# A second pass with results in five half tiles, two sets of down-projection sums made ahead, and memory work dealt out among the attention blocks

## The chip, the cores and the metric

One core of a Trainium2 chip runs the whole kernel. The metric is device time in microseconds (us), the median of the runs. Five engines take part, each with an instruction queue of its own that is worked off in order: PE (TensorE, matmuls), DVE (VectorE), ACT (ScalarE), POOL (GpSimd) and SP (SyncE), which in this kernel issues all the DMAs.

## The reference

One layer of a streaming encoder for 2048 prompt frames and 32 sample frames, width 1024, in float32:

```python
hp = rmsnorm(xp, g_pre_mix)
qa, ka, va, qb, kb, vb, la, r = mix_inputs(hp, w_in, ...)       # one projection
oa = chunk_band_prompt(qa, ka, va, rel_bias)                     # 8 heads x 64, band of 9 chunks
ob, sp = gla_recurrence(qb, kb, vb, la, s0, GLA_BLOCK)           # 4 heads, gated linear attention
xp = xp + rmsnorm(mix_output(oa, ob, r, g_gla_out, w_o), g_post_mix)
mk, mv = mem_kv(mem_prompt, g_mem, w_mk, w_mv)                   # 256 memory rows
xp = xp + rmsnorm(mem_attention(rmsnorm(xp, g_pre_mem), mk, mv, w_mq, w_mo), g_post_mem)
xp = xp + rmsnorm(swiglu(rmsnorm(xp, g_pre_ffn), w_gate, w_up, w_down), g_post_ffn)   # hidden 2816
```

The sample frames go the same way with caches. Keys and values of the memory, the recurrence's states and the last attention keys and values are outputs too.

## The kernel before

**Arithmetic.** A float32 product is made as three products of fp32r halves, hi x hi, hi x lo and lo x hi (`mm3`). `split` makes the halves: ACT casts the high one (L459), DVE or POOL subtracts for the low one (L460); `split_own` does so in place (L464, L465). Large products use a seven-product scheme, so that weights are added and subtracted in sevens ahead of the matmuls.

**Order.** The kernel's instructions are recorded, and `class Order` then plans the issue order of every engine by a list schedule with estimated costs in several passes. The order in which the code is written sets priorities only. What the planner fixes is the order in each engine's queue; at run time each queue waits for what its first instruction needs.

**Stages**, with the time in the profiled execution of before:

- 0 to 535: projections.
- 535 to 1119: band attention and GLA in four blocks of tokens. PE's short attention products are mixed with "dense" steps, taken from a list `dense` with one entry for each block: for block 0 the memory keys (`mkps`) and `keys_fold` of the four memory heads (`gps`), for blocks 1 to 3 the out-projection of the block before (`wops`, which multiplies w_o with `om`, the mixer's output that is stored to `od` and loaded again). A number beside each entry paces its steps.
- 1119 to 1149: the memory values (`vals`: eight groups `mvps` of 24 matmuls, each copied out by DVE as `mvf`, L1510, from the pool `pd`, which has one PSUM bank).
- 1149 to 1231: the last out-projection woven with `values_fold(h)` for the four heads. `values_fold` multiplies the head's values `vt` with pieces of w_mo (`wov`) into `hps`, copies that to `hst` (DVE and ACT in turn, L1555) and stores it to `hd`. Beside it `score_weights` prepares the next stage.
- 1231 to 1405: scores of the memory attention.
- 1405 to 1632: the second pass, `output(i, pT)` for eight tiles of 256 tokens. A tile loads its probabilities `pT`, which are split in place, multiplies them with `hT` (`mo`, 192 matmuls), copies the four banks into `y` (`my`, ACT, L1874), norms, adds x1, stores x2, norms again and stores h2 (`h2d<-my`). The pool "by" has two buffers for y, 8 KB each for a partition, so tile i+2's first copy waits until tile i's last store has landed. Between the tiles `sums_out` makes the FFN's down-projection sums of set 0 (`down_pair(0)`: `wdr` is loaded, added and subtracted, split into `wds`, stored to `wdd`).
- 1632 to 3012: the FFN in three blocks of tokens (`pg`, `pu`, `pdX/Y/Z`). Block 0 makes the sums of the sets that are not in `MADE`, uses them and stores them to `wdd` for the other blocks. Set 4 is made in the projection stage.

The junction between attention and out-projection is a chain: `g_tt` (PE transposes the last GLA outputs), `g_sg` (DVE), the store to `od`, the load of `om` (L1102), ACT's cast and POOL's subtract for each of eight `om`, then `wops`.

The lines that the change speaks of:

```python
dense = [(steps(kv + [partial(keys_fold, h) for h in range(HM)]), 1 + 8 * 2 + 5 * HM), ...]
...
for _ in steps(vals):
    pass
...
for _ in steps(outp[3][0] + weave(outp[3][1], [partial(values_fold, h) for h in range(HM)], lead=1.0)):
    pass
...
yp = pool("by", 2)
y = yp.tile([P, KT, 256], F32, tag="y", name=f"my{i}")
MADE = (0, 4,)
```

Of the kernel before, what the change touches and what calls it, by code (L numbers as in the profile page):

```python
# [9 lines left out]
F32 = mybir.dt.float32  # L10
F32R = mybir.dt.float32r
AF = mybir.ActivationFunctionType
ALU = mybir.AluOpType
# [5 lines left out]
P = 128  # L19
D = 1024  # L20
KT = D // P
# [408 lines left out]
def encoder_step(ctx, tc, ins, outs):  # L430
    nc = tc.nc
    ACT, DVE, POOL, SP = nc.scalar, nc.vector, nc.gpsimd, nc.sync
# [17 lines left out]
    gains = {}  # L450
# [80 lines left out]
    HM = 4  # L531
# [16 lines left out]
    HK = KT // 2  # L548
# [93 lines left out]
    with ExitStack() as ph:  # L642
        def pool(name, bufs, **kw):
            return ph.enter_context(tc.tile_pool(name=name, bufs=bufs, **RW, **kw))
# [7 lines left out]
        wrp = pool("pwr", 4)  # L652
# [374 lines left out]
        bufs = []  # L1027
# [9 lines left out]
        items, raw = quarters(0, True)  # L1037
# [3 lines left out]
        for b in range(len(PB)):  # L1041
# [15 lines left out]
            if b + 1 < len(PB):  # L1057
                items, raw = quarters(b + 1)
# [13 lines left out]
    with ExitStack() as ph, ExitStack() as dn:  # L1072
# [6 lines left out]
        sp = pool("as", 2, dn)  # L1079
# [6 lines left out]
        up = pool("au", 4, att, **RT)  # L1086
        gp = pool("ag", 1, att, **RT)
        pd = pool("apd", 1, space=PSUM)
        pm = pool("apm", 2, apm, space=PSUM)
# [433 lines left out]
        def fold_head(src, h, nm):  # L1523
            t = kvs[-1].tile([P, 2, 544], F32R, tag="xw", name=f"{nm}{h}")[:, :, :512]
            SP.dma_start(t[:, 1].bitcast(F32).rearrange("p (j n) -> p j n", j=2), src[h * 256 : h * 256 + 256, :].rearrange("(j p) n -> p j n", p=P))
            split_own(t, True)
            return t
# [4 lines left out]
        def keys_fold(h):  # L1532
            kt = fold_head(mkd, h, "kt")
            for a in range(2):
                w = fold_w(ins["w_mq_t"], h, a, "wqt")
                for i2 in range(2):
# [7 lines left out]
                    SP.dma_start(gd[a][h // 2].rearrange("p (k n) -> p k n", k=HK)[:, 2 * i2 : 2 * i2 + 2, c0 : c0 + NMEM], g.rearrange("p (i n) -> p i n", i=2))  # L1544
                    yield

        def values_fold(h):
            vt = fold_head(mvd, h, "vt")
            for a in range(2):
                w = fold_w(ins["w_mo"][0], h, a, "wov")  # L1550
                for t in range(2):
                    ps = psc.tile([P, 512], F32, tag="X", name=f"hps{h}{a}{t}", bufs=2)
                    mm3(ps, [((vt[:, 0, j * NMEM + t * P : j * NMEM + t * P + P], vt[:, 1, j * NMEM + t * P : j * NMEM + t * P + P]), (w[j][0][:, 0], w[j][1][:, 0])) for j in range(2)])
                    hv = sp.tile([P, 544], F32, tag="st", name=f"hst{h}{a}{t}")[:, :512]
                    (ACT.copy if t else DVE.tensor_copy)(hv, ps)  # L1555
                    SP.dma_start(hd[(2 * h + t) * P : (2 * h + t + 1) * P, a * 512 : a * 512 + 512], hv)
                    yield


        def steps(items):  # L1560

            for it in items:
                r = it()
                if r is not None:
                    yield from r
                yield
# [27 lines left out]
        fin_at = [0] + [fin_at[4 * b + 3] for b in range(NB - 1)] + [len(order)]  # L1594
        kv, vals = mem_kv()
        outp = [out_proj(b) for b in range(NB)]
        dense = [(steps(kv + [partial(keys_fold, h) for h in range(HM)]), 1 + 8 * 2 + 5 * HM), (steps(outp[0][0] + outp[0][1]), 25), (steps(outp[1][0] + outp[1][1]), 25), (steps(outp[2][0] + outp[2][1]), 25)]
        ends = starts[1:] + [total]
        FIN = {0: (0,), 1: (1, 2), 2: (3, 4), 4: (5,), 5: (6, 7), 6: (8, 9)}
        DSTART, DEND = (6, 4, 7, 7), (0, 0, 0, 7)  # L1600
# [42 lines left out]
            for _ in gen:  # L1643
                pass
        states_out()
        for _ in steps(vals):
            pass
        axs.close()
        att.close()
# [5 lines left out]
        psc = pool("bpc", 1, pss, **RP)  # L1655
# [27 lines left out]
                SP.dma_start(s6d[:, k * 512 : k * 512 + 512], b21)  # L1683

        score_weights()
        for _ in steps(outp[3][0] + weave(outp[3][1], [partial(values_fold, h) for h in range(HM)], lead=1.0)):
            pass
        psx.close()
        amm.close()
# [11 lines left out]
        for i, src in ((5, gd[1][0]), (6, s6d)):  # L1701
            raw = weight_of(i)
# [103 lines left out]
        wrp = pool("bcr", 4, **RT)  # L1806
        hps_ = [pool(f"bh{q}", 1, **RT) for q in range(4)]
        tps = [pool(f"bt{q}", 1, **RT) for q in (2, 3, 0, 1)]
        yp = pool("by", 2)
        sp = pool("bs", 2)  # L1810
        side = Tagged(raw=wrp, sum=pool("bcs", 6), down=pool("bcd", 4))
        spacer("gap1", 4352, left=True)
        side.pools.update(u=pool("bcu", 3), stage=pool("bct", 3))
        pn = pool("bpm", 2, **RP)
# [2 lines left out]
        for q in range(4):  # L1817
            t = hps_[q].tile([P, 2, 2, D], F32R, tag="h", name=f"hT{q}")
# [14 lines left out]

        def output(i, pT):
            t0 = i * 256
            y = yp.tile([P, KT, 256], F32, tag="y", name=f"my{i}")
            pair = lambda m2: y[:, 2 * m2 : 2 * m2 + 2]
            ssq = {}

            def square(m2, nm):  # L1840
                if m2 == 0:
                    ssq[nm] = sp.tile([P, 2, 256], F32, tag="ssq", name=f"{nm}s{i}")
                    ACT.activation(ssq[nm], pair(0), AF.Square)
                else:
                    sq = sp.tile([P, 2, 256], F32, tag="sq", name=f"{nm}q{i}_{m2}")
                    ACT.activation(sq, pair(m2), AF.Square)
                    add(DVE, ssq[nm], ssq[nm], sq)

            def rstd(nm):
                r = (pd.tile([P, 512], F32, tag="dense", name=f"{nm}{i}") if nm == "n3_" else ptr.tile([P, 512], F32, tag="tr", name=f"{nm}{i}"))[:, :256]  # L1850
                add(DVE, ssq[nm][:, 0], ssq[nm][:, 0], ssq[nm][:, 1])
                PE.matmul(r, lhsT=ones, rhs=ssq[nm][:, 0], start=True, stop=True)
                ACT.activation(r, r, AF.Ln, bias=eps_t, scale=1.0 / D)
                ACT.activation(r, r, AF.Exp, scale=-0.5)
                return r

            def store(dst, m2):
                for b, lo, hi, off in pieces(CB, t0, t0 + 256):
                    SP.dma_start(dst[b][2 * m2 * P : (2 * m2 + 2) * P, lo:hi].rearrange("(k p) n -> p k n", p=P), pair(m2)[:, :, off : off + hi - lo])

            def scaled(m, g, r):
                DVE.scalar_tensor_tensor(out=y[:, m], in0=y[:, m], scalar=gains[g][:, m : m + 1], in1=r, op0=ALU.mult, op1=ALU.mult)

            banks = (pn, py) if i == NQ - 1 else pys
            for m4 in range(2):
                pss = [banks[m4].tile([P, 512], F32, tag="norm" if banks[m4] is pn else "out", name=f"mo{i}_{2 * m4 + j}") for j in range(2)]
                for e in range(2):
                    for hf in range(2):
                        for j in range(2):
                            c = slice((4 * m4 + 2 * j + e) * P, (4 * m4 + 2 * j + e) * P + P)  # L1870
                            mm3(pss[j][:, e * 256 : e * 256 + 256], [((hT[hf * HK + k][:, 0, c], hT[hf * HK + k][:, 1, c]), (pT[hf][:, 0, k], pT[hf][:, 1, k])) for k in range(HK)], hf == 0, hf == 1)
                for j in range(2):
                    m2, ps = 2 * m4 + j, pss[j]
                    ACT.copy(pair(m2), ps.rearrange("p (e n) -> p e n", e=2))  # L1874
                    square(m2, "n3_")
            yield
            r = rstd("n3_")
            (b, lo, _, _), = pieces(BLK, t0, t0 + 256)
            for m2 in range(KT // 2):
                xr = sp.tile([P, 2, 256], F32, tag="xr", name=f"x1r{i}_{m2}", bufs=3)  # L1880
                SP.dma_start(xr, x1d[b][2 * m2 * P : (2 * m2 + 2) * P, lo : lo + 256].rearrange("(k p) n -> p k n", p=P))
                for m in (2 * m2, 2 * m2 + 1):
                    scaled(m, "g_post_mem", r)
                add(POOL, pair(m2), pair(m2), xr)
                store(x2d, m2)
                square(m2, "n4_")
            yield
            r = rstd("n4_")
            for m2 in range(KT // 2):
                for m in (2 * m2, 2 * m2 + 1):  # L1890
                    scaled(m, "g_pre_ffn", r)
                store(h2d, m2)
# [94 lines left out]
        def sums_out():  # L1987
            for j in MADE[:-1]:
                yield from (it() for it in down_pair(j, lambda name: [side.tile([P, 2, 512], F32R, tag="down", name=f"{name}_{q}") for q in range(4)], lambda n, name: side.tile([P, 2, 512], F32R, tag="sum", name=name)))

        MADE = (0, 4,)
        own, sums = sample(), sums_out()
        last, pT = None, probs_of(0)
        for i in range(NQ):
# [13 lines left out]
    with ExitStack() as ph:  # L2008
# [4 lines left out]
        uu = pool("cu", UB)  # L2013
        gp = pool("cg", 4)
        np_ = pool("cn", 1)
        xp = pool("cx", 2)
        mps = {i: pool(f"cm{i}", 1) for i in range(7)}
        wr = pool("cwr", WRB, **RT)
# [3 lines left out]
        sp = pool("cs", 4, **RT)  # L2022
# [11 lines left out]
        pd = Turns([pool("cpd0", 3, space=PSUM, **RT), pool("cpd1", 3, space=PSUM)], 3)  # L2034
# [79 lines left out]
        with tc.high_priority(offset=PRI):  # L2114
            raw = {}
# [8 lines left out]
        for b, (s, n) in enumerate(CF):  # L2124
# [40 lines left out]
            def down_sums(j):  # L2165

                w = {}
                with tc.high_priority(offset=PRI):
                    if b or j in MADE:
                        for i in XYZ:  # L2170
# [167 lines left out]
            for g in range(NG):  # L2338
# [3 lines left out]
                if not last and g == NG - 2:  # L2342
                    raw = ffn_raw(b + 1, 0)
# [91 lines left out]
```

## Time and profile before

| what | before |
|---|---|
| median of 3 runs | 3011.1 us (3009.85 to 3013.73) |
| profiled execution | 3014.34 us, span of its instructions 3012.6 us |
| PE busy | 2936.7 us (97%), 20995 matmuls |
| DVE, ACT, POOL busy | 2263.5, 1593.8, 838.3 us |
| mean granted TensorE clock | 0.992 |
| moved by DMA | 578.90 MB, mean 192 GB/s |

Idle time of an engine matters only where the engine that sets the end waits for it. The median and the profiled execution are different executions, so a sum worked out from the trace is set against the trace's own time first.

### The profile page before, as it was taken

Reading aid. Unit: us, or ns where it says so; the run is one execution under the profiler, and the core shown is the slowest. Engines: PE = TensorE matmul, PEld = TensorE weight load, DVE = VectorE, ACT = ScalarE, POOL = GpSimd, SP = SyncE. Lnnn points to the kernel's source line nnn. Section 1 sums busy time; section 2 is a strip of 40 time slices with the busy share of each in tenths; the row PEclk is TensorE's granted clock in tenths of the full one; section 3 lists DMA queues with packets and bytes.
Section 4 is the critical chain, followed back from the end, with each engine's and each line's share of the span. In section 5 each row is a group of like instructions: output and inputs, shape, how many; then the busy total and the mean of one; then the engine's idle time right before and its main releaser. Section 6 shows DMA issues by size and latency. Waiting matters only on the chain.

```text
span 3012.6 us, 56389 instructions
## 1 busy us (share of the span) xinstructions
PE 2936.7 (97%) x20995; PEld 2758.1 (92%) x20995; DVE 2263.5 (75%) x4173; ACT 1593.8 (53%) x3389; POOL 838.3 (28%) x987
## 2 busy tenths in 40 slices
PE   9999999999999998999999999999999999999997
PEld 7899999888887777888989999999999999999997
DVE  6588876566776777874667888889977778977775
ACT  5555555676776665565435544445433335433343
POOL 0201000556767463221221111114211113311113
PEclk9999999999999999999999999999999999999999
DMA  9567374996775769546773544454454445544434
GB/s 319 197 202 239 115 232 154 302 304 196 244 246 187 214 214 313 176 156 220 260 241 112 183 149 155 165 182 162 152 195 129 136 153 174 177 164 139 132 127 169
DMA packets 429636, 578.90 MB, mean 192 GB/s; under 512 B 48720, under 2 KB 321081, under 8 KB 429329
## 3 DMA queue, kind: packets, MB, share of 16 engines
q1 hardware_dynamic: 429361, 575.29, 58.4%
q8 instruction: 165, 2.70, 0.4%
q14 instruction: 110, 0.90, 0.1%
HBM read 419.12 MB, written 160.33 MB: 192 GB/s over the span
## 4 chain that ended last, share of the span: by engine, by line
PE 88%; DMA 4%; DVE 4%; ACT 2%; issue 1%; POOL 1%; SPq 0%; DVEq 0%; ACTq 0%; POOLq 0%
PE pu_X L500 8%; PE pg_X L500 8%; PE pdX L500 8%; PE mo L500 5%; PE wops L1426 5%; PE pu_Y L500 4%; PE pg_Y L500 4%; PE pdY L500 4%; PE msX L500 3%; PE pu_Z L500 2%; PE s L1154 2%; PE pg_Z L500 2%; PE po L1162 2%; PE pdZ L500 2%; PE pt L1182 2%; PE pdn L500 1%
## 5 line engine op out<-in xcount | busy, mean ns | idle before, releaser
L460 POOL TENSOR_TENSOR u<-g,u 128x692 fp32r<-128x692 f32 (+1 forms) x111 | 200.0, 1808 | 901.7 <-ACT u L459 872.7
L500 PE MATMUL pg_X<-mf,wg_s 128*128 128x346 f32 (+1 forms) x1584 | 278.4, 323 | 1.2 <-DVE g L555 1.2
L500 PE MATMUL pu_X<-mf,wu_s 128*128 128x346 f32 (+1 forms) x1584 | 276.5, 322 | 0.9 <-ACT pu_c L638 0.8
L500 PEld LDWEIGHTS pg_X<-mf,wg_s 128*128 128x128 f32 x1584 | 256.8, 189 | 3.3 <-DVE g L555 1.7
L500 PEld LDWEIGHTS pu_X<-mf,wu_s 128*128 128x128 f32 x1584 | 256.7, 189 | 1.6 <-ACT pu_c L638 1.5
L500 PE MATMUL pdX<-u,wd 128*128 128x346 f32 (+1 forms) x1440 | 233.2, 322 | 0.0
L500 PEld LDWEIGHTS pdX<-u,wd 128*128 128x128 f32 x1440 | 230.5, 189 | 0.0
L459 ACT CAST wg_s<-wg_r 128x512 fp32r<-128x512 f32 x231 | 136.2, 620 | 176.0 <-DVE wg_r L552 80.3
L1426 PE MATMUL wops<-om,wo_s 128*128 128x512 f32 (+1 forms) x960 | 215.8, 362 | 8.2 <-ACT wo_s L459 4.7
L459 ACT CAST u<-g 128x692 fp32r<-128x692 f32 (+1 forms) x111 | 84.3, 774 | 221.2 <-PE pdX L500 165.0
L500 PE MATMUL mo<-pT,hT 128*128 128x256 f32 x1536 | 195.2, 287 | 6.0 <-ACT my L1874 3.9
L500 PEld LDWEIGHTS mo<-pT,hT 128*128 128x128 f32 x1536 | 189.2, 194 | 12.6 <-ACT my L1874 4.9
L460 DVE TENSOR_TENSOR wu_s<-wu_r,wu_s 128x512 fp32r<-128x512 f32 x231 | 172.8, 774 | 25.7 <-ACT wu_s L459 25.5
L460 DVE TENSOR_TENSOR wg_s<-wg_r,wg_s 128x512 fp32r<-128x512 f32 x231 | 160.6, 718 | 34.1 <-ACT wg_s L459 34.0
L459 ACT CAST wu_s<-wu_r 128x512 fp32r<-128x512 f32 x231 | 136.7, 620 | 88.2 <-DVE wu_r L552 37.3
L1426 PEld LDWEIGHTS wops<-om,wo_s 128*128 128x128 f32 x960 | 152.6, 189 | 30.9 <-ACT wo_s L459 5.7
L500 PE MATMUL pg_Y<-mf,wg_s 128*128 128x346 f32 (+1 forms) x792 | 139.0, 322 | 4.9 <-ACT my L1874 3.2
L500 PE MATMUL pu_Y<-mf,wu_s 128*128 128x346 f32 (+1 forms) x792 | 138.1, 322 | 2.4 <-ACT wu_s L459 2.4
L555 DVE TENSOR_TENSOR acc<-acc,pdX 128x346 f32<-128x346 f32 (+1 forms) x192 | 96.9, 513 | 57.4 <-PE pdX L500 57.2
L500 PEld LDWEIGHTS pg_Y<-mf,wg_s 128*128 128x128 f32 x792 | 128.1, 189 | 6.1 <-ACT my L1874 3.5
L500 PEld LDWEIGHTS pu_Y<-mf,wu_s 128*128 128x128 f32 x792 | 128.0, 188 | 3.1 <-ACT wu_s L459 3.0
L1341 POOL TENSOR_TENSOR g_W<-g_W,g_kq 128x128 f32<-128x128 f32 x224 | 108.6, 519 | 56.2 <-ACT g_W L1333 55.9
(561 smaller groups left out, 7186.1 us busy)
## 6 DMA issues: line engine op xcount, KB each, us to landing
wd<-wdd SPq DMA_DIRECT2D x168, 512.0 KB, 5.3
wg_r<-in_w_ffn_gate_dram SPq DMA_DIRECT2D x66, 512.0 KB, 4.2
wu_r<-in_w_ffn_up_dram SPq DMA_DIRECT2D x66, 512.0 KB, 4.6
wdd<-wd SPq DMA_DIRECT2D x42, 512.0 KB, 3.2
q<-qd SPq DMA_DIRECT2D x32, 512.0 KB, 5.4
wo_r<-in_w_o_dram SPq DMA_DIRECT2D x64, 256.0 KB, 3.8
nb<-nbd SPq DMA_DIRECT2D x16, 640.0 KB, 7.3
ks<-kad SPq DMA_DIRECT2D x20, 512.0 KB, 6.5
```

The source lines that it names most:

```text
L459: ACT.copy(hi, src)
L460: (lo_eng or DVE).tensor_tensor(out=lo, in0=src, in1=hi.bitcast(F32), op=ALU.subtract)
L500: PE.matmul(ps, lhsT=a, rhs=b, start=first and i == 0, stop=last and i == len(seq) - 1, skip_group_check=skip)
L555: eng.tensor_tensor(out=out, in0=a, in1=b, op=ALU.add)
L1154: PE.matmul(ps_out, lhsT=q[:, 2 * i + e, q0 : q0 + nq], rhs=ks[:, e, k0 : k0 + ncol], start=i == 0, stop=i == 1)
L1162: PE.matmul(po[e * 64 : e * 64 + 64, :n], lhsT=v[:kk, j, e * 64 : e * 64 + 64], rhs=prts[e][:kk, j, :n], start=j == 0, stop=j == len(rows) ...
L1182: PE.transpose(ptp[:kk, j, :n], pr[:n, c0 : c0 + kk], ident[:n, :n])
L1341: POOL.tensor_tensor(out=wl, in0=wl, in1=both, op=ALU.mult)
L1426: PE.matmul(ps, lhsT=a, rhs=b, start=i == 0, stop=i == len(seq) - 1)
```

## The change

- The dense steps are dealt anew: block 0 gets the memory keys and `keys_fold` of heads 0 and 1 (27 steps to pace by), block 1 the first out-projection and `keys_fold` 2 (30), block 2 the second and the memory values (42), block 3 the third and `keys_fold` 3 (30).
- After attention, `values_fold` of heads 0 and 1 stand where the memory values stood. For these heads `fold_bank` takes attention's PSUM banks (`pm` for t = 1, `pd` for t = 0) and the staging comes from attention's pool `up`. The last out-projection is woven with heads 2 and 3 alone.
- y is two half tiles of 4 KB a partition each, from a pool of five; the pool of finished sums goes from six to five.
- `MADE` is (0, 1, 4): set 1 is made in the second pass, and FFN block 0 loads it.
- A spacer of 328 floats stands in the FFN's pools.

```diff
+        def fold_bank(h, t, name):
+            if h in [0, 1]:
+                return (pm if t else pd).tile([P, 512], F32, tag="gla" if t else "dense", name=name)
+            return psc.tile([P, 512], F32, tag="X", name=name, bufs=2)
+
         def values_fold(h):
...
-                    ps = psc.tile([P, 512], F32, tag="X", name=f"hps{h}{a}{t}", bufs=2)
+                    ps = fold_bank(h, t, f"hps{h}{a}{t}")
...
-                    hv = sp.tile([P, 544], F32, tag="st", name=f"hst{h}{a}{t}")[:, :512]
+                    hv = (up.tile([P, 640], F32, tag="sb", name=f"hst{h}{a}{t}") if h in [0, 1] else sp.tile([P, 544], F32, tag="st", name=f"hst{h}{a}{t}"))[:, :512]
...
-        dense = [(steps(kv + [partial(keys_fold, h) for h in range(HM)]), 1 + 8 * 2 + 5 * HM), (steps(outp[0][0] + outp[0][1]), 25), (steps(outp[1][0] + outp[1][1]), 25), (steps(outp[2][0] + outp[2][1]), 25)]
+        dense = [(steps(kv + [partial(keys_fold, 0)] + [partial(keys_fold, 1)]), 27), (steps(outp[0][0] + outp[0][1] + [partial(keys_fold, 2)]), 30), (steps(outp[1][0] + outp[1][1] + vals), 42), (steps(outp[2][0] + outp[2][1] + [partial(keys_fold, 3)]), 30)]
...
-        for _ in steps(vals):
+        for _ in steps([partial(values_fold, 0)] + [partial(values_fold, 1)]):
...
-        for _ in steps(outp[3][0] + weave(outp[3][1], [partial(values_fold, h) for h in range(HM)], lead=1.0)):
+        for _ in steps(outp[3][0] + weave(outp[3][1], [partial(values_fold, 2)] + [partial(values_fold, 3)], lead=1.0)):
...
-        yp = pool("by", 2)
+        yp = pool("by", 5)
         sp = pool("bs", 2)
-        side = Tagged(raw=wrp, sum=pool("bcs", 6), down=pool("bcd", 4))
+        side = Tagged(raw=wrp, sum=pool("bcs", 5), down=pool("bcd", 4))
...
-            y = yp.tile([P, KT, 256], F32, tag="y", name=f"my{i}")
-            pair = lambda m2: y[:, 2 * m2 : 2 * m2 + 2]
+            y = [yp.tile([P, HK, 256], F32, tag="y", name=f"my{i}_{j}") for j in range(2)]
+            pair = lambda m2: y[m2 // 2][:, m2 % 2 * 2 : m2 % 2 * 2 + 2]
...
-        MADE = (0, 4,)
+        MADE = (0, 1, 4,)
...
+        pool("cgap", 1).tile([P, 328], F32, name="cgap")
```

Three places show what the planner made of this. In the rows, a name before the arrow is the tile written, the names behind it are those read; xN counts alike instructions in a row.

PE before, at the junction: ahead of these rows stand the last `g_tt` and four more groups mvps of 24 matmuls, all behind it; these are the last of them and the first rows of the last out-projection.

```order
L1426 MATMUL mvps_15542<-mv_15251,wmv_0_s 128x256 x6
L1426 MATMUL mvps_15542<-mv_15253,wmv_0_s 128x256 x6
L1426 MATMUL mvps_15542<-mv_15255,wmv_4_s 128x256 x6
L1426 MATMUL mvps_15542<-mv_15257,wmv_4_s 128x256 x6
L1426 MATMUL wops_0_0_15751<-om_4_15704,wo_0_4_s 128x272 x2
L1426 MATMUL wops_0_1_15777<-om_4_15704,wo_0_4_s 128x272 x2
L1426 MATMUL wops_0_0_15751<-om_4_15704,wo_0_4_s 128x272
L1426 MATMUL wops_0_0_15751<-om_5_15708,wo_0_4_s 128x272 x3
```

PE after, at the same place:

```order
L1413 MATMUL g_tt<-ident,g_ob 128x128 x4
L500 MATMUL hps_15595<-wov_s,vt_15571 128x512 x6
L500 MATMUL hps_15625<-wov_s,vt_15571 128x512 x6
L500 MATMUL hps_15659<-wov_s,vt_15635 128x512 x6
L500 MATMUL hps_15689<-wov_s,vt_15635 128x512
L500 MATMUL hps_15649<-wov_s,vt_15635 128x512 x6
L500 MATMUL hps_15689<-wov_s,vt_15635 128x512 x5
L500 MATMUL hps_15679<-wov_s,vt_15635 128x512 x6
L1426 MATMUL wops_0_0_15879<-om_4_15832,wo_0_4_s 128x272 x3
L1426 MATMUL wops_0_0_15879<-om_5_15836,wo_0_4_s 128x272 x3
L1426 MATMUL wops_0_0_15879<-om_6_15840,wo_0_4_s 128x272 x3
```

Behind `g_tt`, 120 matmuls of mvps have given way to 36 of hps; wops_0_0 then runs through all eight om before wops_0_1 begins.

ACT before, at the junction (`om` are the casts that POOL's subtracts wait for, `vt` the values of a head):

```order
L464 CAST om_4_15704<-om_4_15704 128x544
L464 CAST om_5_15708<-om_5_15708 128x544
L459 CAST wmv_4_s<-wmv_4_r 128x512
L464 CAST om_6_15712<-om_6_15712 128x544
L464 CAST om_7_15716<-om_7_15716 128x544
L464 CAST vt_15804<-vt_15804 128x512
L459 CAST wo_0_0_s<-wo_0_0_r 128x512
L459 CAST wo_0_4_s<-wo_0_4_r 128x512
L459 CAST wov_s<-wov_r 128x512
```

ACT after, at the junction:

```order
L459 CAST wov_s<-wov_r 128x512 x2
L1560 COPY hst_15632<-hps_15625 128x512
L459 CAST wo_0_0_s<-wo_0_0_r 128x512
L464 CAST om_4_15832<-om_4_15832 128x544
L459 CAST wo_0_4_s<-wo_0_4_r 128x512
L464 CAST om_5_15836<-om_5_15836 128x544
L464 CAST om_6_15840<-om_6_15840 128x544
L464 CAST om_7_15844<-om_7_15844 128x544
L1560 COPY hst_15666<-hps_15659 128x512
```

The cast of w_o's piece, which needs a buffer that hps read, now stands ahead of om_4's, behind the copies of two hps.

ACT before, in the second pass (`my_19594` is tile 4's y, `my_20148` tile 6's, `n_4_20131` tile 4's second norm):

```order
L464 CAST pT_1_20364<-pT_1_20364 128x1024
L1846 ACTIVATE n_q_2_20119<-my_19594 128x512
L1846 ACTIVATE n_q_3_20128<-my_19594 128x512
L459 CAST mf_2_20853<-acc_20838 128x1392
L1853 ACTIVATE n_4_20131<-n_4_20131,eps_t 128x256
L1854 ACTIVATE n_4_20131<-n_4_20131 128x256
L1874 COPY my_20148<-mo_0_20149 128x512
L1843 ACTIVATE n_s_20248<-my_20148 128x512
L1874 COPY my_20148<-mo_1_20150 128x512
```

ACT after, in the second pass (`my_0_20226` and `my_1_20227` are tile 6's halves, `n_4_20209` is tile 4's second norm):

```order
L1880 COPY my_0_20226<-mo_0_20228 128x512
L1880 COPY my_0_20226<-mo_1_20229 128x512
L1848 ACTIVATE n_s_20180<-my_0_19626 128x512
L1851 ACTIVATE n_q_1_20188<-my_0_19626 128x512
L1851 ACTIVATE n_q_2_20197<-my_1_19627 128x512
L1851 ACTIVATE n_q_3_20206<-my_1_19627 128x512
L1851 ACTIVATE n_q_1_20330<-my_0_20226 128x512
L459 CAST mf_3_20940<-acc_20923 128x1392
L459 CAST mf_4_20943<-acc_20923 128x1392
L1858 ACTIVATE n_4_20209<-n_4_20209,eps_t 128x256
L1859 ACTIVATE n_4_20209<-n_4_20209 128x256
```

The copies of tile 6's first half have moved ahead of tile 4's second norm; the second half's first copy comes four rows further on, behind a norm of tile 5.

More of the change, by code (lines that the diff above doesn't have):

```diff
@@ L1861, in scaled @@
             def scaled(m, g, r):
-                DVE.scalar_tensor_tensor(out=y[:, m], in0=y[:, m], scalar=gains[g][:, m : m + 1], in1=r, op0=ALU.mult, op1=ALU.mult)
+                v = y[m // HK][:, m % HK]
+                DVE.scalar_tensor_tensor(out=v, in0=v, scalar=gains[g][:, m : m + 1], in1=r, op0=ALU.mult, op1=ALU.mult)
             banks = (pn, py) if i == NQ - 1 else pys
```

## Prediction

> **What bounds the kernel now.** I read the page first: the busy shares, the granted clock by slice and the shares of the chain that ended last.
>
> ```profile
> span 3012.6 us, 56389 instructions
> PE 2936.7 (97%) x20995; PEld 2758.1 (92%) x20995; DVE 2263.5 (75%) x4173; ACT 1593.8 (53%) x3389; POOL 838.3 (28%) x987
> PE 88%; DMA 4%; DVE 4%; ACT 2%; issue 1%; POOL 1%; SPq 0%; DVEq 0%; ACTq 0%; POOLq 0%
> ```
>
> PE is busy 97% of the span and has 12% of the chain against it. The change leaves the 20995 matmuls as they are, tile by tile, so the most that it can win is the idle 3012.6 - 2936.7 = 76 us and what PE does at a low clock. So the next view is a table of stretches, PE's busy time against their length: the last half of attention block 2, the end of attention, the memory values alone, the last out-projection, the output stage, the first two stretches of the FFN.
>
> ```profile
> 944.00:982.00 38.00, 32.73 (x323) 25.95 (x323) 25.36 (x66) 28.44 (x72) 35.27 (x37) 0.96 0.79 250
> 1106.00:1128.00 22.00, 18.27 (x156) 15.24 (x155) 16.25 (x39) 11.99 (x39) 14.16 (x15) 0.84 0.66 199
> 1128.00:1161.00 33.00, 27.70 (x187) 24.98 (x185) 21.85 (x31) 15.64 (x26) 14.42 (x10) 0.95 0.96 324
> 1161.00:1231.00 70.00, 63.77 (x417) 57.93 (x416) 55.73 (x82) 38.37 (x71) 13.50 (x9) 0.98 0.74 244
> 1405.00:1632.00 227.00, 220.69 (x1740) 206.46 (x1739) 139.12 (x226) 94.91 (x170) 60.77 (x33) 0.98 0.71 231
> 1632.00:1728.00 96.00, 86.78 (x511) 84.27 (x510) 84.13 (x138) 60.59 (x107) 13.09 (x9) 0.95 0.48 152
> 1728.00:1890.00 162.00, 162.00 (x1016) 162.00 (x1015) 142.06 (x230) 72.80 (x134) 29.14 (x16) 1.00 0.47 164
> ```
>
> Columns: length, busy time of PE, weight loads, DVE, ACT, POOL, then granted clock, DMA share, GB/s. Idle PE in order: 5.27, 3.73, 5.30, 6.23, 6.31, 9.22 and 0. The clock falls below 1 where PE waits; slices of 5 us show by how much:
>
> ```profile
> 965.00:970.00 5.00, 4.89 (x36) 4.08 (x37) 1.37 (x6) 2.94 (x7) 5.00 (x5) 0.66 0.33 114
> 1115.00:1120.00 5.00, 2.55 (x13) 1.87 (x14) 3.65 (x9) 1.26 (x2) 4.92 (x7) 0.60 0.82 255
> 1120.00:1125.00 5.00, 5.00 (x28) 4.52 (x28) 2.47 (x5) 1.59 (x6) 0.73 (x1) 0.72 0.39 118
> 1145.00:1150.00 5.00, 4.76 (x28) 4.79 (x29) 3.20 (x4) 2.48 (x4) 3.58 (x3) 0.67 0.99 357
> 1580.00:1585.00 5.00, 3.51 (x16) 3.51 (x17) 4.31 (x4) 4.12 (x8) 1.61 (x1) 0.52 1.03 337
> 1585.00:1590.00 5.00, 5.00 (x36) 5.00 (x35) 3.98 (x4) 4.39 (x7) 2.41 (x1) 0.79 0.47 160
> 1640.00:1645.00 5.00, 3.71 (x11) 3.26 (x12) 4.93 (x9) 4.55 (x11) 0.00 (x0) 0.50 0.42 122
> ```
>
> Busy time times the missing clock is what a slice lost: 4.89 x .34 = 1.7; 1.0 + 1.4; 1.6; 1.7 + 1.1; 1.9. PE's waits in its timeline (start, length, and in brackets the idle time ahead and its releaser) say what each followed:
>
> ```profile
> 965.11 0.73 PE L1426 MATMUL wops<-om,wo_s 128*128 128x512 f32 x2 [1.92 <-POOL om L465]
> 1127.75 0.60 PE L1413 MATMUL g_tt<-ident,g_ob 128*128 128x128 f32 x4
> 1132.12 3.07 PE L1426 MATMUL mvps<-mv,wmv_s 128*128 128x256 f32 x24 [0.61 <-DVE mvf L1510]
> 1145.24 4.23 PE L1426 MATMUL mvps<-mv,wmv_s 128*128 128x256 f32 x24 [2.70 <-DVE mvf L1510]
> 1149.27 2.95 PE L1426 MATMUL wops<-om,wo_s 128*128 128x272 f32 x19
> 1163.04 1.66 PE L500 MATMUL hps<-wov_s,vt 128*128 128x512 f32 x6 [1.20 <-ACT hst L1555]
> 1180.27 2.95 PE L500 MATMUL hps<-wov_s,vt 128*128 128x512 f32 x12
> 1553.14 15.86 PE L500 MATMUL mo<-pT,hT 128*128 128x256 f32 x130 [1.47 <-ACT my L1874]
> 1579.03 0.50 PE L500 MATMUL mo<-pT,hT 128*128 128x256 f32 x2 [1.42 <-ACT pT L464]
> 1581.49 13.61 PE L500 MATMUL mo<-pT,hT 128*128 128x256 f32 x91 [1.96 <-ACT my L1874]
> 1636.81 2.65 PE L500 MATMUL pg_Y<-mf,wg_s 128*128 128x348 f32 x12 [3.21 <-ACT my L1874]
> ```
>
> Each low slice follows a wait of 1.5 to 3.2 us. So a wait of that size costs its own length and about 1.5 us behind it.
>
> **The change part by part.** The sum is made against the profiled execution, 3014.3 us (span 3012.6), which lies 3.2 above the median of 3011.1.
>
> *A, fillers in attention.* In the order of before, PE has up to 17 us of attention's own short products between two dense fillers, 14 in the stretch 944-982; in the new order none is over 7.5 us (both by the pace of such matmuls in the trace). At stake are the idle and the lost clock of 944-982 and 1106-1128: 5.27 + 1.7 + 3.73 + 2.4 = 13. The wait at 965 is for POOL's om, which the filler does not speed up, and the tail at 1115 keeps its chain; what remains waits for DVE and is what a filler covers. I take -8; ends 0 and -13.
>
> *B, memory values.* Eight groups mvps move into attention block 2. Behind each other they hand over one bank: the wait of 0.61 stands three times (1132.12 and two like it), then 2.70 and 1.6 of clock: -6.1. Between attention products DVE's copy is covered. The cover if that fails is again the bank; ends -6.1 and -3.
>
> *C, the junction.* The chain from g_tt over the store to od, the load of om, ACT's cast and POOL's subtract to the first wops is not changed:
>
> ```profile
> L1102 SPq DMA_DIRECT2D om<-od x8: 382/446/651, 1135.0 to 1151.2; - x8
> L465 POOL TENSOR_TENSOR om<-om x8: 1336/1363/1814, 1140.4 to 1158.7; 128x544 fp32r<-128x544 f32 x8
> DMA to landing us min/median/max: 4.4/5.0/6.6
> ```
>
> First POOL om comes at 1140.4, 12.7 us behind g_tt. Before, five mvps of 3.07 us and their waits fill the time to 1149.27, by when several om are ready. After, three head-steps of hps stand there, 36 matmuls; at 12 in 2.95 us they are 8.9 us of work. Then comes wops_0_0 alone, k by k, each of its eight om made by POOL one behind the other: 12.7 + 8 x 1.36 = 23.6, and 0.4 for the last three matmuls: it ends 24 us behind g_tt. PE has 0.6 + 8.9 + 3.1 (24 matmuls at the 3.07/24 of mvps) = 12.6 of work there. So 11.4 idle and 1.5 of clock: +13. Low end +6: od and om land some 3 us earlier, since the loads of w_mo have been made and the DMA share (0.96 in 1128-1161) falls, POOL at 1336, and no clock is lost. High end +19: in ACT's new order om_4's cast stands behind wo_0_0's, whose buffer comes free only with an hps that waits for a bank; about 4.5 us later, with 1.5 of clock more. I take the middle, as nothing excludes either.
>
> By the Trainium skill, "GPSIMD Engine Reference", 1 Specifications, GpSimd shares SBUF interfaces with VectorE and contends with DVE instructions that have two SBUF inputs, such as the subtracts of `split`. The trace agrees in that the same om takes 1336 to 1814 ns; with all eight at 1814 C would be +16.6.
>
> *D, two heads less woven into the last out-projection.* Of 1161-1231's idle 6.23 us, hand-overs like that at 1163.04 are the larger part. Half of the hps leave, but the out-projection's own weight casts stay. I take -2; ends 0 and -5.
>
> *E, half tiles of y.* What the buffers cost:
>
> ```profile
> DMA h2d<-my: 13.4, 3
> PE mo L500: 3.9, 3
> PE pg_Y L500: 3.2, 1
> ```
>
> Of ACT's copies into my, three sat 13.4 us until the store of the tile two earlier had landed; PE's mo waited 3.9 and the first FFN products 3.2 for those copies. Five halves are 20 KB where two wholes were 16: half a tile more of room. In ACT's new order tile 6's first two copies stand ahead of tile 4's norm, before they stood behind it; the second half's still stands behind. At stake are 3.9 + 3.2, the 1.42 at 1579.03 that has pT's cast behind a waiting copy, and 4.7 of clock: 13. I take -9, two thirds. Ends -13 and +3 (pT's cast stands later in ACT's queue).
>
> *F, the second set of sums.* It leaves FFN block 0 and joins the output stage. The set that is there already, and its stretch:
>
> ```profile
> L459 ACT CAST wds<-wdr x14: 602/616/625, 1430.5 to 1455.7; 128x512 fp32r<-128x512 f32 x14
> L460 DVE TENSOR_TENSOR wds<-wdr,wds x14: 676/684/694, 1431.2 to 1456.3; 128x512 fp32r<-128x512 f32 x14
> L608 SPq DMA_DIRECT2D wdd<-wds x14: 319/335/905, 1431.9 to 1461.6; - x14
> DMA to landing us min/median/max: 5.5/6.1/8.4
> 1430.00:1462.00 32.00, 32.00 (x265) 29.88 (x264) 21.14 (x29) 16.91 (x29) 2.49 (x1) 1.00 0.99 364
> ```
>
> A set is 14 x 0.62 = 8.6 us of ACT, 14 x 0.68 and the eight sums of `down_pair`, taken at the same size, on DVE = 15.0, and 18 DMAs of 512 KB = 9.4 MB, all issued from SP's one queue, past pT, x1 and the stores of h2d. In 1405-1632 DVE goes from 139 to 154 of 227 us and the transfers from 231 to 272 GB/s. Set 0 was made at a DMA share of 0.99 and 364 GB/s with PE busy 32.00 of 32.00 us. Where it leaves, PE is busy 162.00 of 162.00 us: nothing to win. Block 0 now loads the 14 pieces. I take 0; ends -2 (block 0's first tail in 1632-1728) and +6 (one pT late by a set's landing time). One buffer of sums less (five for six) lies in the +6. The spacer of 328 floats moves addresses alone: 0.
>
> Sum: -8 - 6.1 + 13 - 2 - 9 + 0 = -12.1, so 3002.2 for the profiled execution and 2999 for the median.
>
> By the Trainium skill, "TensorE: Matmul & The Clock Gate", What's actually happening, the clock halves only after an idle window of about 3.4 us, in a window that runs freely. The rows differ: 1.92 us of wait precede a slice at 0.66. By the rule the clock shares in A, B, C and E would not follow the waits: about 1.5 less in A and B each, 3 less in E and 1.5 less loss in C, which makes 3004.
>
> **The rivals.**
>
> *A wash.* The junction takes what the values gave. Speaks for it: five mvps stood there as cover and nothing of their length replaces them. With C at +19, D 0, E -5, A -8, B -6.1, F 0 it is 3014.2, on the median 3011. Against it: that ACT's cast is late by so much needs the bank hand-over to take longer than the 1.20 seen at 1163.04.
>
> *Slower: the transfers of the second set.* Place: tiles 4 to 6 of the output stage. A tile of 192 mo is 23 us (130 in 15.86 at 1553.14); its reload of pT, x1 and the store of h2d must land in that. The DMA share is already 1.03 at 1580-1585, 337 GB/s. The set's 9.4 MB take 28 us at that rate. If they fall where the share is near 1, half of that comes out on PE, +14, and E is lost: -8 - 6.1 + 13 - 2 + 0 + 14 = +11, on the median 3022. It decides from the point at which the round trip of y passes a tile's 23 us. Against it: the mean share is 0.71, and the full DMA engines of 1430-1462 left no PE wait, though no tile of y was then waiting for its buffer.
>
> *Full gain.* The halves remove all waits and the junction is short: C +6, E -13, the rest as taken: -23, on the median 2988.
>
> **How the numbers follow.** Forecast (2992 to 3005) 0.50, full gain 0.13, wash 0.21, transfers 0.10, other losses 0.06. From no change this kernel's measurement tells about 0.2%, 6 us: under 3005 is faster, over 3017 slower. Faster: 0.50 + 0.13 less the forecast's upper edge 0.01 = 0.62; same: the wash but for its upper tail, 0.20 and that edge, 0.21; slower 0.17. The range leaves out the transfers, most of other losses and the lower part of full gain: 2984 to 3014.
>
> **What would show it.** A: no PE wait over 1.5 us in the stretches of fillers, clock at 0.95 or more there. B: no mvf as releaser of 0.61. C: in the 24 us behind the last g_tt, PE 11 us idle with POOL om or ACT om as releaser, and a slice at 0.6 to 0.7. D: one or two waits for hst fewer. E: "DMA h2d<-my" below 5 us among ACT's copies, the wait at the first pg_Y gone. F: no mo wait for pT over 1.5 us, 1728-1890 still full. The prediction is wrong if om's cast in ACT is late by far more than the bank, or if mo's waits stay with another releaser (pT, or the banks).

## The result, and the profile after

The changed kernel takes 3001.5 us at the median of 8 runs (2997.0 to 3007.7); the kernel before took 3012.3 in the 8 runs beside it. The ratio is 0.9968, 95% interval 0.9959 to 0.9977: 10 us faster, where 2999 was forecast. The page of the changed kernel, first its span, the engines' busy times and the chain that ended last:

```profile
span 3001.3 us, 56406 instructions
PE 2932.2 (98%) x20995; PEld 2755.9 (92%) x20995; DVE 2259.3 (75%) x4173; ACT 1591.5 (53%) x3388; POOL 836.1 (28%) x987
PE 91%; DMA 3%; DVE 3%; ACT 1%; POOL 1%; issue 1%; SPq 0%; DVEq 0%; ACTq 0%; POOLq 0%
```

The total came out as forecast, its parts did not. Cut both traces at the same matmuls (first mkps, first msX, first mo, first pg_X, first pdX, and the first pg_X and the first pdX of block 1); msX to mo, 175 us in both, is left out. First the table of before, then that of after (columns as in the prediction):

```profile
536.40:1231.40 695.00, 669.06 (x6773) 569.51 (x6772) 496.76 (x1286) 471.72 (x1293) 403.33 (x688) 0.99 0.77 243
1406.70:1631.30 224.60, 218.29 (x1728) 204.40 (x1727) 137.66 (x225) 92.82 (x167) 60.53 (x33) 0.98 0.71 231
1631.30:1727.80 96.50, 87.28 (x513) 84.73 (x512) 84.24 (x139) 61.29 (x107) 13.09 (x9) 0.95 0.48 150
1727.80:2095.60 367.80, 365.98 (x2281) 364.00 (x2281) 324.98 (x524) 166.09 (x302) 77.56 (x46) 1.00 0.49 168
2095.60:2181.40 85.80, 82.87 (x511) 80.77 (x510) 78.17 (x114) 47.10 (x87) 25.90 (x21) 1.00 0.43 135
```

```profile
536.40:1235.30 698.90, 672.02 (x6774) 571.28 (x6773) 499.85 (x1288) 469.98 (x1294) 401.10 (x688) 0.98 0.76 242
1410.60:1625.50 214.90, 214.16 (x1727) 201.80 (x1726) 151.59 (x245) 103.79 (x185) 62.94 (x33) 1.00 0.84 283
1625.50:1722.20 96.70, 86.57 (x515) 83.85 (x513) 83.72 (x142) 57.65 (x102) 11.15 (x8) 0.95 0.46 141
1722.20:2088.70 366.50, 364.76 (x2281) 363.85 (x2281) 307.92 (x502) 160.07 (x291) 78.21 (x47) 1.00 0.49 167
2088.70:2171.00 82.30, 81.63 (x511) 80.65 (x510) 72.45 (x110) 46.18 (x84) 23.50 (x20) 1.00 0.48 149
```

Attention to out-projection: 3.9 us longer. Second pass: 9.7 shorter, with PE idle for 0.74 us of 214.90. Start of the FFN: as before, though its old waits are gone. The rest of FFN block 0 and the start of block 1: 1.3 and 3.5 shorter, with 17 and 6 us less of DVE. PE's waits in the timeline of after, two at the junction, two in the last out-projection, one in the FFN:

```profile
1154.05 5.77 PE L500 MATMUL hps<-wov_s,vt 128*128 128x512 f32 x17 [2.01 <-DVE hst L1560]
1168.23 1.05 PE L1426 MATMUL wops<-om,wo_s 128*128 128x272 f32 x3 [0.70 <-POOL om L465]
1187.18 3.15 PE L500 MATMUL hps<-wov_s,vt 128*128 128x512 f32 x12 [2.36 <-ACT g L459]
1192.90 17.78 PE L1426 MATMUL wops<-om,wo_s 128*128 128x272 f32 x140 [2.08 <-DVE wo_s L460]
1699.20 3.85 PE L500 MATMUL pu_X<-mf,wu_s 128*128 128x348 f32 x12 [7.67 <-DVE up L555]
```

Of the waits that the prediction listed in the second pass and at the first FFN products none is left. Of ACT's copies into my two still sat for a store, 5.2 us against 13.4, and PE waited for none of them:

```profile
L1880 ACT COPY my<-mo x32: 565/585/602, 1428.2 to 1635.4; 128x512 f32<-128x512 f32 x32
  DMA h2d<-my: 5.2, 2
```

In their place stands 7.67 us at 1699, where PE waits for `up`, DVE's sum of two `pu` results; the largest wait for `up` in this stretch of before was 2.49 us. In the trace of after DVE works off the norms of tiles 6 and 7 among the FFN's first sums there.

### The profile page after: what moved, and what is told of

It reads as the page before. It is cut to its first block, busy times and chain, and to the rows that moved or that the text cites. A ratio compares the mean times of both kernels' runs of the same rounds, so it can differ in the third digit from the quotient of the medians.

```text
span 3001.3 us, 56406 instructions
## 1 busy us (share of the span) xinstructions
PE 2932.2 (98%) x20995; PEld 2755.9 (92%) x20995; DVE 2259.3 (75%) x4173; ACT 1591.5 (53%) x3388; POOL 836.1 (28%) x987
## 4 chain that ended last, share of the span: by engine, by line
PE 91%; DMA 3%; DVE 3%; ACT 1%; POOL 1%; issue 1%; SPq 0%; DVEq 0%; ACTq 0%; POOLq 0%
PE pu_X L500 8%; PE pg_X L500 8%; PE pdX L500 8%; PE mo L500 6%; PE wops L1426 6%; PE pu_Y L500 4%; PE pg_Y L500 4%; PE pdY L500 4%; PE msX L500 3%; PE s L1154 2%; PE pu_Z L500 2%; PE po L1162 2%; PE pg_Z L500 2%; PE pdZ L500 2%; PE pt L1182 2%; PE pdn L500 2%
```

## The experiments

Each ran in five rounds beside the kernel before; ratios are to it. First each part by itself.

**Attention part alone** (`att_only`): the diff's edits to `dense`, `fold_bank`, `values_fold` and the two lists behind attention, nothing else.

> The kernel before with the attention part of the change alone (fillers dealt anew, memory values in block 2, two heads' folds behind attention). Theory, from the two traces: from the first memory keys to the first scores the changed kernel takes 698.9 us where before took 695.0, since the junction's waits of about 1 us each bring six slow clock windows; so this is 3 to 5 us slower than before, 3015 to 3017. Rival 1, the prediction's sum of A to D: 3 us faster, 3008 to 3009. Rival 2, one profile's chance: no difference within 2 us.

Measured: 1.0011 (1.0002 to 1.0020), 3016.1 against 3012.1. First memory keys to first scores take 699.0 us in its trace. The theory holds, and the prediction's sum of A to D had the wrong sign; a difference of under 2 us, the second rival, is not excluded by the interval.

**Half tiles alone** (`y_only`):

```diff
-        yp = pool("by", 2)
+        yp = pool("by", 5)
-        side = Tagged(raw=wrp, sum=pool("bcs", 6), ...
+        side = Tagged(raw=wrp, sum=pool("bcs", 5), ...
```

with y in two halves as in the change, and no spacer.

> The kernel before with y in five half tiles and five sum buffers alone. Theory: mo's waits for ACT's copies go (6.3 us idle and 3.4 of clock in the second pass), the second pass falls from 224.6 to about 215 us, and of the 5 us at the first FFN products about nothing is kept, since DVE is late there in its place: 9 to 10 us faster. Rival 1: the copies' wait only turns into a wait for pT or for DVE's norms, 3 to 5 us faster. Rival 2: with the wait at the first FFN products gone too and DVE less full than in the changed kernel, 13 to 15 us faster.

Measured: 1.0036 (1.0023 to 1.0049), 3023.2: 11 us slower, outside all three. No copy of ACT holds PE any more, but PE now waits up to 8.63 us for the norms ahead of the first FFN product. What is left out beside the other two parts is the spacer; `no_spacer` and `y_spacer` below test it.

**Set 1 alone** (`made_only`): `MADE = (0, 1, 4,)` in the kernel before.

> The kernel before with set 1 of the sums made in the second pass alone, y as two whole tiles. Theory: its 9.4 MB and 15 us of DVE delay the stores that y's buffers wait for, so the second pass gets 2 to 5 us longer, and FFN blocks 0 and 1 win 3 to 5 us back (1.4 and 3.4 in the changed kernel's trace): within 2 us of before. Rival 1, the prediction's F: nothing anywhere. Rival 2, the prediction's rival of the transfers: 10 us slower or more.

Measured: 1.0027 (1.0017 to 1.0038), 3020.5, 8 us slower. The second pass grew from 224.6 to 237.3 us, and these are its largest waits, in PE's timeline:

```profile
1538.95 15.47 PE L500 MATMUL mo<-pT,hT 128*128 128x256 f32 x105 [5.56 <-ACT my L1874]
1595.93 11.11 PE L500 MATMUL mo<-pT,hT 128*128 128x256 f32 x76 [3.28 <-ACT pT L464]
1652.12 3.85 PE L500 MATMUL pg_Y<-mf,wg_s 128*128 128x348 f32 x12 [7.41 <-ACT my L1874]
```

So the mechanism of the prediction's slow rival is real: the set's work and transfers delay y's stores (ACT's copies into y wait 19.4 us for them in this trace, 13.4 in that of before), and two whole buffers of y hand that to PE. It cost 13 us in the second pass, more than twice the theory's upper end, and the rest of block 0 and the start of block 1 gave 4.5 back, as the theory had it (1.3 and 3.2; block 1's start took 82.5 us). So the total lies between the theory and that rival.

**Four halves, no more room** (`y_four_halves`): as `y_only` with `pool("by", 4)` and six sum buffers, so that no address moves.

> The kernel before with y in four half tiles and six sum buffers, so with no more room than two whole tiles have. Theory: it is the finer hand-over that counts, since a half is free as soon as its own two stores have landed: two thirds or more of what five halves bring, 6 to 10 us faster. Rival: it is the extra half tile of room that counts, and four halves bring 0 to 3 us.

Measured: 1.0023 (1.0014 to 1.0032), 3019.0, 7 us slower. The second pass wins 1.4 us, then one wait loses it all:

```profile
1644.51 3.85 PE L500 MATMUL pg_Y<-mf,wg_s 128*128 128x348 f32 x12 [16.41 <-ACT my L1875]
```

In ACT's timeline the copy that PE waits for sat 9.80 us itself until a store of h2 had landed and a half was free:

```profile
1643.87 1.07 ACT L1875 COPY my<-mo 128x512 f32<-128x512 f32 x2 [9.80 <-DMA h2d<-my]
```

Finer hand-over alone does not pay; the rival was nearer, with a wrong sign.

The three parts alone, the halves without the spacer, are slower, 3.4 + 11 + 8, and all together they are 10 us faster. So there are interactions, and the next kernels leave parts out of the changed one.

**Without the spacer** (`no_spacer`): the changed kernel without `pool("cgap", 1)`.

> The changed kernel without the spacer of 328 floats in the FFN's pools. Theory: the spacer keeps the FFN's first mf off the memory of y's last half tile; without it the planner sets all the norms of tiles 6 and 7 ahead of the first FFN product, as in y_only, and PE waits there for the norm chain with some 25 us idle and 14 of slow clock; the FFN's first products then run with fewer waits. The second pass goes from 215 to 235 to 245 us, the next stretch from 96.6 to about 87: 10 to 20 us slower than the changed kernel, 3011 to 3021. Rival, the prediction: a spacer moves addresses alone, no difference.

Measured: 1.0035 (1.0022 to 1.0049), 3021.6, which is 20 us above the changed kernel, at the theory's upper end; the second pass takes 244.3 us and the next stretch 86.6. The rival, the prediction's own "0", is off by that much. The loads of the FFN's first operand show it best, first in after, then without the spacer (the two times are the first and the last issue):

```profile
L2126 SPq DMA_DIRECT2D acc<-h2d x4: 666/1134/1245, 1540.1 to 1566.8; - x4
```

```profile
L2125 SPq DMA_DIRECT2D acc<-h2d x4: 487/525/776, 1643.3 to 1645.0; - x4
1628.65 1.22 PE L1857 MATMUL n<-n_s,ones 128*128 128x256 f32 x2 [6.22 <-DVE n_s L555]
1634.17 1.22 PE L1857 MATMUL n<-n_s,ones 128*128 128x256 f32 x2 [4.30 <-DVE n_s L555]
1644.02 1.22 PE L1857 MATMUL n<-n_s,ones 128*128 128x256 f32 x2 [8.63 <-DVE n_s L555]
1649.80 0.66 PE L500 MATMUL pg_X<-mf,wg_s 128*128 128x348 f32 x1 [4.56 <-ACT mf L459]
```

With the spacer the loads of `acc` are issued 59 to 85 us ahead of the first FFN product, without it only 5 to 7 us ahead, behind the last stores of x2 in SP's queue. The same is seen in `y_only` (1643.4 us), and in no other kernel here. In the planner's order PE's four last norms then stand ahead of the first pg_X. That it is the memory of y's last halves that `acc` waits for is inferred from which edits move it (five halves with five sum buffers, and a shift of 1312 bytes); the addresses themselves were not read.

**Halves and spacer** (`y_spacer`): `y_only` with the spacer.

> The kernel before with y in five half tiles, five sum buffers and the spacer, without set 1 in the second pass and without the attention part. Theory: with the spacer the loss of y_only is gone and the waits for ACT's copies too: second pass 214 to 216 us, next stretch about 96, so 8 to 11 us faster than before, 3001 to 3004. Rival: y_only's loss came from the halves themselves (more stores in SP's queue), and this is as slow as y_only, 3020 to 3024.

Measured: 0.9978 (0.9966 to 0.9989), 3003.7 against 3010.1. Second pass 214.8 us, the next stretch 96.6, so the theory's stage times hold. The median's 6.5 us is below its 8 to 11; in the trace the rest of FFN block 0 gives some of the gain back, 370.4 us against 367.8. This is term E.

**Without the attention part** (`no_att`): halves, spacer and set 1.

> The changed kernel without the attention part (fillers, memory values and folds as before; y halves, set 1 and spacer as changed). Theory, by att_only's +3.4: 3 to 5 us faster than the changed kernel, 2996 to 2999. Rival, the prediction's A to D: 3 us slower than the changed kernel, 3004 to 3005.

Measured: 0.9955 (0.9942 to 0.9968), 2996.8: the fastest median here, 13 us below before and by ratio 4 below the changed kernel, though their intervals overlap. Against `y_spacer` set 1 is worth 0.0023 or 7 us, where alone in the kernel before it cost 8.

**A third head at the junction** (`three_heads`):

```diff
-        for _ in steps([partial(values_fold, 0)] + [partial(values_fold, 1)]):
+        for _ in steps([partial(values_fold, h) for h in range(3)]):
```

with `if h in [0, 1, 2]` for the banks and head 3 alone woven.

> The changed kernel with values_fold of head 2 too behind attention (in attention's banks), so that 24 more hps, 5.9 us at 12 in 2.95, can stand between g_tt and the first wops, and head 3 alone is woven later. Theory: the junction's eight waits for POOL's om are short cover; 6 us more of it takes 4 to 6 us of idle and some of the slow clock: 4 to 8 us faster than the changed kernel, 2994 to 2998. Rival: the waits only move, since the hand-over of the one bank pd (wait for DVE's hst, 2.0 us in the changed kernel) comes more often and the woven part loses a head as filler: within 2 us of the changed kernel.

Measured: 0.9965 (0.9952 to 0.9978), 3000.0. The waits for POOL's om are gone, and others stand there:

```profile
1152.24 6.00 PE L500 MATMUL hps<-wov_s,vt 128*128 128x512 f32 x18 [2.91 <-DVE hst L1560]
1161.24 1.67 PE L500 MATMUL hps<-wov_s,vt 128*128 128x512 f32 x6 [0.85 <-DVE hst L1560]
1166.39 1.67 PE L500 MATMUL hps<-wov_s,vt 128*128 128x512 f32 x6 [1.64 <-DVE hst L1560]
1169.74 0.51 PE L1426 MATMUL wops<-om,wo_s 128*128 128x272 f32 x2 [1.68 <-ACT wo_s L459]
```

The rival holds: cover that hands over one bank waits for that bank.

**Keys alone dealt anew** (`keys_dealt`): `no_att` with `keys_fold` 2 and 3 in blocks 1 and 3.

> no_att (0.9955 of before) with one half of the attention part: the folds of the memory keys of heads 2 and 3 move from block 0 to blocks 1 and 3, while the memory values stay behind attention and all four heads' value folds stay woven. Theory: filler there ends waits for DVE but the large wait of that stretch was for POOL's om and the tail at 1115 keeps its chain, so 0 to 3 us faster than no_att. Rival, the prediction's A of -8: 6 us or more faster. Second rival: block 0 now lacks filler, 2 us or more slower.

Measured: 0.9960 (0.9948 to 0.9972), 2998.5: no difference from `no_att` that can be told, and not the 6 us or more of the rival. The wait for POOL's om that before has at 965 is not there, and the stretch has others in its place:

```profile
963.20 0.55 PE L1182 MATMUL pt<-ident,u_sb 128*128 128x128 f32 x3 [1.07 <-ACT u_sb L1141]
974.13 0.77 PE L1388 MATMUL g_o<-gla_state,g_cq 128*128 128x256 f32 x2 [1.67 <-ACT acc L1457]
```

**Values split** (`split_values`): `vals[:5]` in block 2, `[vals[0]] + vals[5:]` and head 0's fold behind attention, three heads woven.

> The changed kernel with only four of the eight value groups in block 2; the other four stand behind attention (their rows are loaded a second time), then the fold of head 0, and three heads are woven. Between g_tt and the first wops stand about 9 us of mvps and 5.9 of hps in place of 8.9 of hps. Theory: cover of 15 us against a chain of 12.7 to the first om, so the waits of 0.66 to 0.80 for POOL's om shrink and fewer slow windows follow: 2 to 6 us faster than the changed kernel, 2996 to 3000. Rival: as with the third head, the one bank's hand-overs (mvf, hst) take the place of those waits, within 2 us of the changed kernel.

Measured: 0.9966 (0.9952 to 0.9979), 2999.3. No om wait is left at the junction, but mvf takes 3.81 us at 1139.63 and a cast of wo_s 2.98 at 1171.16. The rival holds by the ratio; 2 us of gain cannot be excluded.

**Norms on POOL** (`norms_pool`, and then `norm7_pool` for the last tile alone), both on `no_att`:

```diff
-                    add(DVE, ssq[nm], ssq[nm], sq)
+                    add(POOL if i > NQ - 3 else DVE, ssq[nm], ssq[nm], sq)
```

> no_att with the twelve sums of squares of the last two tiles of the second pass on POOL in place of DVE. Theory: the 7.7 us wait at 1696 (for DVE's up) stems from DVE working off the norms of tiles 6 and 7 among the FFN's first sums; 12 x 0.7 = 8 us less for DVE there, at 1.3 us each on an engine that is idle there, takes 3 to 6 us of that wait and of the slow clock behind it: 2991 to 2994. Rival: the norms' own chain gets longer on POOL and the wait only moves, within 2 us of no_att.

> no_att with the six sums of squares of the last tile alone on POOL. In norms_pool the copies of tile 7 into y waited for a half tile whose store came later (PE's pu_X waited 4.5 us for ACT's copy), since tile 6's norm had got slower on POOL. Theory: no buffer waits for tile 7's norm, so with it alone DVE has 6 x 0.7 = 4 us less among the FFN's first sums and the 7.7 us wait for up shrinks by 2 to 4 us, with nothing given back: 2992 to 2995. Rival: the wait for up does not hang on these sums but on the planner's order of DVE at that place, within 2 us of no_att or slower.

Measured: 0.9976 (0.9967 to 0.9985), 3002.9, by ratio 6 us slower than `no_att`, though the intervals touch; and 0.9954 (0.9941 to 0.9967), 2997.9, the same as it. Both theories' gains failed to come. With tile 7 alone the wait for up is 4.22 in place of 7.70, as that theory had it, but a wait for ACT's copy that `no_att` does not have has taken the difference:

```profile
1640.20 3.85 PE L500 MATMUL pu_X<-mf,wu_s 128*128 128x348 f32 x12 [3.85 <-ACT my L1875]
1696.61 3.20 PE L500 MATMUL pu_X<-mf,wu_s 128*128 128x348 f32 x12 [4.22 <-DVE up L555]
```

How to win the 10 us of PE's idle at the start of the FFN stays open.

## Why the prediction was right in total and wrong in its parts

| step | forecast | measured |
|---|---|---|
| A to D, attention to out-projection | -3.1 | +3.4 (`att_only`), +3.9 in the trace |
| E, halves, with the spacer | -9 | -6.5 (`y_spacer`), -9.6 in the trace |
| spacer | 0 | 20 without it |
| F, set 1 | 0 | -7 beside the halves, +8 alone |
| sum | -12.1 | -10 |

**A** is the step that failed first. It took the idle time and lost clock of two stretches, 13 us, for what fillers can cover, and let them have 8. From the first memory keys to the last g_tt PE's idle was 14.4 us before (first row) and is 15.2 after (second row, 18 us longer by the work that moved in):

```profile
536.40:1128.10 591.70, 577.28 (x6172) 486.29 (x6170) 419.28 (x1176) 417.41 (x1198) 375.41 (x669) 0.99 0.76 239
```

```profile
536.40:1146.30 609.90, 594.68 (x6306) 502.78 (x6304) 434.36 (x1194) 423.37 (x1210) 375.56 (x671) 0.99 0.76 241
```

The work that moved in accounts for the 18 us (120 of `mvps` at 3.07 us for 24 and 12 of `hps` at 2.95 are 18.3), so nothing was won. The wait of 1.92 us for POOL's om at 965 is gone, and the two longest waits for another engine in this stretch of after, the first of which before does not have, are for ACT (`prt` is its copy of transposed probabilities):

```profile
986.30 0.44 PE L1182 MATMUL pt<-ident,u_sb 128*128 128x128 f32 x2 [3.52 <-ACT prt L1184]
1001.45 0.50 PE L1332 MATMUL gs_e<-tall,gs_laR 32*128 32x256 f32 x2 [1.56 <-ACT acc L1457]
```

The keys' part alone (`keys_dealt`) brings nothing either. The longest runs of short products, read from an order, do not say what PE waits for there: it waits for single results of other engines, and other filler moved which.

**B** was right: in the changed kernel PE waits for no mvf. With A at 0, B at -6.1, C at +10.8 and D at -1, as measured below, the stretch comes to +3.7, and its trace says +3.9.

**C** was right in mechanism and near in size. These stretches of after hold the end of attention, the junction and the last out-projection:

```profile
1126.00:1146.70 20.70, 17.69 (x137) 12.30 (x134) 16.12 (x36) 14.01 (x45) 18.53 (x18) 0.86 0.73 227
1146.70:1172.00 25.30, 18.79 (x65) 13.53 (x66) 16.81 (x21) 12.10 (x21) 12.23 (x8) 0.77 0.95 332
1172.00:1235.30 63.30, 58.15 (x405) 54.89 (x405) 48.68 (x73) 34.14 (x63) 13.31 (x9) 0.98 0.69 219
```

The second is 25.3 us, where 24 were forecast, with 6.5 idle: 3.9 for POOL's om, and 2.0 for DVE's hst, the hand-over of a bank that the sum did not have. At a clock of 0.77 its 18.8 us of busy time lost another 4.3. That is 10.8 against 13 forecast, with less idle (11.4 forecast) and more lost clock (1.5 forecast). The cast of wo_0_0 ahead of om's did not bring the high end.

**D** was about right: 5.15 us idle in the third row against 6.23.

**E** took two thirds of 13 us. In the second pass all came, 9.7, and at the first FFN products nothing, since the 7.67 us for up took the place of what went. The step that failed under it is "the spacer moves addresses alone: 0". In the runs that spacer decides whether the FFN's first loads are issued at 1540 us or at 1643, most likely because the FFN's tiles are laid over the second pass's. The range for E had +3 as its bad end; without the spacer it is +11.

**F** was mis-sized because it looked for a gain only in the stretch that had no wait, 1728-1890. The gain came after it, at the start of block 1: 82.3 to 82.5 us in all nine kernels with set 1, 85.6 to 85.8 in all five without. DVE was busy there 78.17 of 85.80 us, 91%; with 17 us less of sums before it, it comes there ahead. Of PE's waits there, two for ACT's cast of wu_s and one of 0.51 us for DVE's wg_s, none is left in after; these are the two of before:

```profile
2110.81 0.58 PE L500 MATMUL pu_Y<-mf,wu_s 128*128 128x346 f32 x2 [1.35 <-ACT wu_s L459]
2167.69 0.58 PE L500 MATMUL pu_Y<-mf,wu_s 128*128 128x346 f32 x2 [1.05 <-ACT wu_s L459]
```

That DVE's lead is the link is argued from these rows and was not tried. Of the 7 us beside the halves, the traces of `no_att` and `y_spacer` show 3.3 here and 4.9 in the rest of block 0, less 1.7 in the second pass. The price that the prediction put into the rival, y's round trip passing a tile's time, was paid nearly in full without the halves (12.7 us of 14) and not with them: the second pass takes 214.9 us in after and 214.8 in `y_spacer`.

So the forecast of 2999 was met because A's missing 8 us and F's 7 us offset each other, and because the change held a spacer that the prediction had at nothing: that the total came out is luck. The rival of a wash rested on C at its high end, which did not come; the rival of the transfers had the right place, but its loss comes only without the halves.

## What to carry to other kernels

Parts of a change may each be slower alone and faster together: more transfers need the buffers that absorb them, and more buffers need the next stage's tiles laid clear of them. Cost a buffer's address like a wait: ask which later load takes the same memory, and when it could otherwise start. A part can also lose in either company, and the total of the change hides it: the attention part cost 3 us in `att_only`, and `no_att` is 4 us below the changed kernel, with intervals that overlap. And do not take a stretch's idle time for what filler can win; first name what each wait there is for, since cover that passes through one bank brings a wait of its own.

## What the runs showed of the clock

Cut into slices of 3.4 us along the edges where it changes, the clock of after is full or half and nothing between (the prediction's 0.66 to 0.79 were means over both):

```profile
1151.25:1154.64 3.39, 1.38 (x6) 0.69 (x5) 3.39 (x7) 0.24 (x1) 0.00 (x0) 1.00 0.86 247
1154.66:1158.06 3.40, 3.40 (x10) 2.62 (x9) 2.85 (x5) 2.16 (x4) 0.82 (x1) 0.50 1.03 386
1158.08:1161.47 3.39, 3.12 (x15) 2.05 (x13) 1.50 (x1) 3.20 (x7) 3.39 (x3) 1.00 1.08 372
1161.49:1164.88 3.39, 1.42 (x8) 0.99 (x8) 1.44 (x1) 2.32 (x4) 3.39 (x4) 1.00 1.07 401
1164.90:1168.30 3.40, 1.90 (x7) 1.26 (x7) 2.08 (x2) 0.00 (x0) 3.40 (x3) 0.50 1.05 397
1168.31:1171.71 3.40, 2.62 (x8) 1.98 (x9) 1.04 (x2) 0.58 (x1) 1.16 (x1) 0.50 1.05 372
1171.72:1175.12 3.40, 3.40 (x16) 3.40 (x16) 0.47 (x1) 1.12 (x2) 0.00 (x0) 0.50 0.99 240
```

In these rows a slice in which PE was busy for 1.4 of 3.4 us is followed by one at half; at half, 2.62 of busy was not enough to end it, 3.40 was. So waits of 0.66 to 0.80 us, one behind the other, bring the low clock as one of 2 us does. The busy share of a slice does not settle it everywhere: in `no_att` 1.66 of 3.40 us at 1164.10 were followed by a slice at full, 2.22 of 3.41 at 1116.27 by one at half, and so was a slice at 1488.33 that is busy throughout, mostly with short matmuls of 128x32. What else counts stays open. The Trainium skill, "TensorE: Matmul & The Clock Gate", What's actually happening, has the two states and a window of 3413 ns that runs freely, and the trace agrees. It lets the clock fall after an idle window; here windows with 1.38 and 1.42 us of work in them were enough.

Where the edges fall differs between executions of the same program part, and with it the time: from the first memory keys to the first scores PE's order is the same in before and in the kernels without any of the attention part, and they take 690.0 (`norms_pool`) to 695.0 us (before). With the attention part the order is again the same in after, `att_only` and `no_spacer`, and they take 699.0, 699.0 and 694.5 us. The 3.9 us of that stretch would not have carried a verdict by themselves; the five rounds of `att_only` do.
